# Loading the history rows of a causal convolution on a second queue, with the column shift folded into the PSUM copies and the first nodes reordered

## Chip, cores, metric

One core of one Trainium2 chip. The metric is device time in microseconds (us) of one execution; lower is better. Each kernel was run several times, and the profiled execution's length is called its span. A program on one core has no neighbour die to compare with, so every run listed here counts as a normal, fast one.

## The reference

`x` is 8 x 4096 x 512 and `kernel` 8 x 512 x 512, both fp32. The output is a causal convolution whose taps are matrices:

```python
for k in range(K):                     # K = 8
    shifted = x if k == 0 else np.concatenate(
        [np.zeros((B, k, D)), x[:, :-k, :]], axis=1)
    out += np.matmul(shifted, kernel[k])
```

## The kernel before

The 32768 rows are laid out as 128 partitions with runs of 256 consecutive rows. A block is eight rows of every run. The eight taps are not multiplied one by one: a three-level Karatsuba-like scheme splits a block into nodes LO, HI and MID and works with sums of rows (VectorE, in bf16) and differences of weights, so that TensorE has few products to do. At full clock a 128x128x512 matmul takes 0.216 us from start to start (1391 of them fill the 300 us from 100 to 400 us of the profile), and four make one "product".

The first block needs, besides its own rows, the seven rows before each run: the *history*. They are the last seven rows of the run in the partition before. The kernel before loads them already moved by one partition, with a cast to bf16 in GpSimd's DMA, and clears partition 0:

```python
def load(out, src):
    nc.gpsimd.dma_start(out=out, in_=src)          # "L80": casts fp32 -> bf16
...
H = D421
def load_h(a, b):
    load(H[1:P, 8 + a:8 + b], xr[0:P - 1, RUN + a:RUN + b, :])
load_h(-4, 0)
load_x(0, 0)
...
nc.vector.memset(H[0:1], 0.0)
...
load_w(4)
load_h(-7, -4)
...
transpose_pe("h0", 0, H, 4, 6)                     # through TensorE into PSUM
transpose_pe("x0", 2, xin[0, 0], 0, 2)
nc.vector.tensor_copy(out=XF[:, 4:6], in_=bank["x0"])
nc.vector.tensor_copy(out=XF[:, 0:2], in_=bank["h0"])
```

Later blocks come in through `load_x` (GpSimd, into one of two `xin` buffers) and `transpose_x` (a DMA transpose on SyncE's queue). A buffer of `xin` is free again when its transpose has read it, so the time of a transpose sets the time of a later load. The transpose in turn waits for VectorE to have read the old contents of `XT` (among others in `prep_d27`).

The first nodes, 0 to 5, do the first two blocks in an order of their own and are written out by hand, followed by the loop from node 6 on. The parts that matter later:

```python
mpool = ctx.enter_context(tc.tile_pool(name="m", bufs=2))       # two "ms" buffers
...
def node_e(n, b_):
    p = n.p[b_]
    if n.k < 4:                      # blocks 0 and 1: LO and HI come first, MID is added later
        pool, name = ((ypool, "y"), (mpool, "ms"), (ypool, "y"), (fpool, "f"))[n.k]
        y = pool.tile([P, 2, D], f32, name=name)
        nc.scalar.copy(out=y, in_=p)
        first[n.i, n.a, b_] = y      # summed and stored from this buffer by node_y and store
    elif n.a == MID:                 # the loop: MID comes first and is kept in ms
        ms[b_] = mpool.tile([P, 2, D], f32, name="ms")
        nc.scalar.copy(out=ms[b_], in_=p)
    ...
```

So node 1's results stay in the two `ms` buffers until their stores, of 512 KB each, have landed. The first `ms` copy of the loop (node 6) must wait for the first of those stores.

In the profile, L76 is the helper of all VectorE sums, L80 GpSimd's load.

## Time and profile before

| quantity | before |
|---|---|
| time, median of 3 runs | 782.44 us (782.19 to 783.35) |
| span of the profiled execution | 779.7 us |
| TensorE busy | 767.2 us |
| VectorE busy | 660.4 us |
| first product | at 13.44 us |

A kernel whose TensorE is busy 98% of the span can gain only where TensorE stands still or its granted clock (1.00 is full speed) is lowered. A line of the timeline gives start, length, engine, line, what; in brackets the idle time before it and what ended it. The table by stretches of the kernel before (from:to, length, then busy us and instructions of PE, PEld, DVE, ACT and POOL, then TensorE's clock, the DMA share and GB/s):

```profile
60.00:100.00 40.00, 39.95 (x185) 17.73 (x184) 38.37 (x48) 14.71 (x25) 1.58 (x3) 1.00 0.77 202
```

TensorE is full there. But the timeline of the same stretch (start, length, engine, line, what; in brackets the idle time before it and what ended it) has one transfer with little to spare:

```profile
77.29 0.33 SPq L276 DMA_DIRECT2D out_dram<-ms  x1
...
77.67 0.53 POOL L80 DMA_DIRECT2D xin<-in_x_dram  x1 [14.40 <-DMA XT<-xin]
...
82.18 1.01 ACT L293 COPY ms<-pp 128x1024 f32<-128x1024 f32 x1 [1.11 <-PE pp L191]
```

The store of `ms` is issued at 77.29, the load of a coming block 0.4 us **behind** it at 77.67. The view of transfers for 74.8 to 79 us says how long the store took (name, queue, count, KB each, us from issue to landing):

```profile
out_dram<-ms SPq DMA_DIRECT2D x1, 512.0 KB, 4.8
```

It landed at 77.29 + 4.8 = 82.1 us, and the copy that takes over the buffer starts at 82.18. By the profile this copy's last wait was for TensorE, not for the store; but a store landing more than 0.1 us later would have held it up.

### The profile page before, as it was taken

What the parts mean: (1) busy time and instruction counts of PE and PEld (TensorE: products, weight loads), DVE (VectorE), ACT (ScalarE), POOL (GpSimd) and SP (SyncE); (2) the same over time, 40 slices, a digit from 0 to 9 for tenths busy, and PEclk for the clock granted to TensorE, in tenths of its full rate; (3) what the DMA queues carried; (4) which work ended last, traced back from release to release, by engine and by line L of the source; (5) the groups of instructions that cost most, each with busy time, mean ns of one, the idle gap of its engine ahead of it and who ended that gap; (6) DMA issues with size and microseconds to landing.
All of it is one profiled execution on the core that took longest, in us unless ns stands there. A gap on an engine that the chain in (4) does not pass through costs nothing.

```text
span 779.7 us, 9419 instructions
## 1 busy us (share of the span) xinstructions
PE 767.2 (98%) x3576; PEld 347.6 (45%) x3576; DVE 660.4 (85%) x768; ACT 280.8 (36%) x459; POOL 41.8 (5%) x80
## 2 busy tenths in 40 slices
PE   6999999999999999999999999999999999999997
PEld 3444444444444444444444444444444444444443
DVE  3999988898888898888898888888888898888895
ACT  1453443324343333343333343333343333343332
POOL 4000000000000000000000000000000000000000
PEclk8999999999999999999999999999999999999999
DMA  9946888777788777687788787878697867688843
GB/s 162 210 80 169 236 189 189 186 168 178 171 176 203 176 180 180 168 193 185 166 192 176 170 198 178 198 161 185 166 190 181 202 162 186 165 186 179 205 131 124
DMA packets 159229, 138.37 MB, mean 177 GB/s; under 512 B 130130, under 2 KB 134226, under 8 KB 159184
## 3 DMA queue, kind: packets, MB, share of 16 engines
q1 hardware_dynamic: 145312, 98.84, 46.0%
q0 software_dynamic: 13728, 38.66, 30.9%
q8 instruction: 28, 0.46, 0.2%
q10 hardware_dynamic: 144, 0.26, 0.1%
q14 instruction: 17, 0.14, 0.1%
HBM read 77.32 MB, written 67.11 MB: 185 GB/s over the span
## 4 chain that ended last, share of the span: by engine, by line
PE 93%; DVE 5%; DMA 1%; issue 1%; ACT 0%; POOL 0%; DVEq 0%; POOLq 0%
PE pp L191 93%; DVE w L76 3%; DVE D L76 1%; DMA xin<-in_x_dram 1%; PE pp L180 0%; DVE pp L76 0%; DVE XT L375 0%; DVE F L76 0%; ACT D L341 0%; ACT D L342 0%; DVE D L334 0%; DVE y L76 0%; DVE pp L266 0%; POOL D L80 0%; DVEq L628 0%
## 5 line engine op out<-in xcount | busy, mean ns | idle before, releaser
L191 PE MATMUL pp<-w,D 128*128 128x512 bf16 x3280 | 718.1, 380 | 1.5 <-ACT D L342 1.1
L191 PEld LDWEIGHTS <-D 128*128 128x128 bf16 x3280 | 320.7, 98 | 391.5 <-issue 4.1
L76 DVE TENSOR_TENSOR D<-D 128x1024 bf16<-128x1024 bf16 x252 | 228.3, 945 | 0.4 <-issue 0.2
L76 DVE TENSOR_TENSOR y<-pp,ms 128x1024 f32<-128x1024 f32 (+1 forms) x121 | 146.2, 1211 | 45.3 <-PE pp L191 45.3
L76 DVE TENSOR_TENSOR D<-XT 128x2048 bf16<-128x2048 bf16 (+2 forms) x153 | 142.3, 945 | 12.2 <-DMA XT<-xin 11.0
L238 ACT COPY pp<-pp 128x512 f32<-128x512 f32 x95 | 54.1, 570 | 254.8 <-PE pp L191 254.8
L250 ACT COPY pp<-pp 128x512 f32<-128x512 f32 x95 | 54.2, 571 | 164.2 <-PE pp L191 154.5
L76 DVE TENSOR_TENSOR pp<-dts,pp 128x512 f32<-128x512 f32 x95 | 65.5, 689 | 43.1 <-ACT dts L256 41.8
L293 ACT COPY ms<-pp 128x1024 f32<-128x1024 f32 x60 | 61.0, 1016 | 33.8 <-PE pp L191 32.8
L80 POOL DMA_DIRECT2D xin<-in_x_dram x64 | 33.9, 530 | 688.0 <-DMA XT<-xin 672.8
L266 DVE SCALAR_TENSOR_TENSOR pp<-pp,dts 128x512 f32<-128x512 f32 x95 | 65.8, 693 | 3.3
L256 ACT COPY dts<-pp 128x512 f32<-128x512 f32 x95 | 57.5, 606 | 4.2 <-PE pp L191 4.2
L252 ACT ACTIVATE pp<-pp 128x512 f32<-128x512 f32 x95 | 56.0, 589 | 2.1 <-DVE D L76 2.1
L191 PE MATMUL pp<-w,XT 128*128 128x512 bf16 x120 | 30.8, 379 | 0.0
L76 DVE TENSOR_TENSOR w<-w,w 128x2048 bf16<-128x2048 bf16 x19 | 22.6, 1218 | 0.0
L191 PEld LDWEIGHTS <-XT 128*128 128x128 bf16 x120 | 11.7, 98 | 14.2
L191 PE MATMUL pp<-w,w 128*128 128x512 bf16 x36 | 9.2, 379 | 0.7 <-ACT pp L250 0.7
L191 PE MATMUL pp<-w,F 128*128 128x512 bf16 x36 | 8.6, 379 | 0.0
L174 PE MATMUL pp<-zero 128*128 128x512 bf16 x16 | 5.6, 501 | 1.2 <-DVE zero L145 1.2
L180 PE MATMUL pp<-ident,xin 128*128 128x128 bf16 x48 | 3.3, 219 | 3.3 <-DMA xin<-in_x_dram 1.9
L334 DVE COPY D<-pp 128x1024 bf16<-128x1024 bf16 x1 | 0.7, 692 | 6.7 <-PE pp L180 6.7
L80 POOL DMA_DIRECT2D w<-in_kernel_dram x8 | 6.0, 758 | 3.0 <-DMA w<-in_kernel_dram 1.9
(52 smaller groups left out, 68.9 us busy)
## 6 DMA issues: line engine op xcount, KB each, us to landing
out_dram<-y SPq DMA_DIRECT2D x123, 512.0 KB, 3.2
xin<-in_x_dram POOLq DMA_DIRECT2D x64, 512.0 KB, 5.7
w<-in_kernel_dram POOLq DMA_DIRECT2D x8, 512.0 KB, 17.2
out_dram<-ms SPq DMA_DIRECT2D x2, 512.0 KB, 6.0
out_dram<-f SPq DMA_DIRECT2D x2, 512.0 KB, 8.4
XT<-xin SPq DMA_TRANSPOSE x61, 6.1
D<-in_x_dram POOLq DMA_DIRECT2D x1, 508.0 KB, 5.5
D<-in_x_dram POOLq DMA_DIRECT2D x1, 381.0 KB, 11.3
```

The lines of the kernel that those rows point to most:

```text
L76: nc.vector.tensor_tensor(out=o, in0=a, in1=b, op=op)
L80: nc.gpsimd.dma_start(out=out, in_=src)
L174: nc.tensor.matmul(pw[:, h], lhsT=zero[:, 0:P], rhs=zero, start=True, stop=True)
L180: nc.tensor.transpose(o[:, t - t0, c * P:(c + 1) * P], src[:, t, c * P:(c + 1) * P], ident)
L191: nc.tensor.matmul(bank, lhsT=comp[:, c * P:(c + 1) * P], rhs=w[:, c, :], start=start and c == 0, stop=c == DC - 1, skip_group_check=True)
L238: nc.scalar.copy(out=n.q[:, 0], in_=n.q[:, 1])
L250: nc.scalar.copy(out=n.p[b_][:, 1], in_=n.q[:, 1])
L252: nc.scalar.mul(out=n.p[b_][:, 1], in_=n.q[:, 1], mul=-1.0)
L256: nc.scalar.copy(out=n.dts, in_=n.q[:, 0])
L266: nc.vector.scalar_tensor_tensor(out=p[:, 0], in0=p[:, 1], scalar=-1.0, in1=n.dts, op0=MUL, op1=SUB)
L293: nc.scalar.copy(out=ms[b_], in_=p)
L334: nc.vector.tensor_copy(out=XF[:, 4:6], in_=bank["x0"])
```

## The change

The intent is a shorter opening. The history's four nearest rows go to SyncE's free queue, so that GpSimd can issue `x` first. That queue's load here stays fp32, so the cast moves to VectorE and ScalarE. The rows are loaded into the same partition that they lie in (no offset, no clearing of partition 0), and the move to the next column is made while the transposes are copied out of PSUM. The order of the hand-written part, nodes 0 to 6, is redone as well. The loop is untouched. The core of the diff, cuts marked:

```diff
-    H = D421
-    def load_h(a, b):
-        load(H[1:P, 8 + a:8 + b], xr[0:P - 1, RUN + a:RUN + b, :])
-    load_h(-4, 0)
+    H, HF = XT, D421.bitcast(f32).rearrange("p (t b) d -> p t (b d)", b=2)
+    nc.sync.dma_start(out=HF, in_=xr[:, RUN - 4:RUN, :])
     load_x(0, 0)
 ...
-    nc.vector.memset(H[0:1], 0.0)
 ...
-    load_h(-7, -4)
+    load(H[:, 1:4], xr[:, RUN - 7:RUN - 4, :])
 ...
+    def to(z):
+        return z.rearrange("p t (c m) -> p t c m", m=P)[:, :, :, 1:P]
+    def prev(z):
+        return z.rearrange("p t (c m) -> p t c m", m=P)[:, :, :, 0:P - 1]
 ...
-    transpose_pe("h0", 0, H, 4, 6)
+    nc.vector.tensor_copy(out=H[:, 4:6], in_=HF[:, 0:2])
+    nc.scalar.copy(out=H[:, 6:8], in_=HF[:, 2:4])
+    n0.p = {0: pair(0), 1: pair(1)}
+    load_w(6)
+    transpose_pe("h0", 3, H, 4, 6)
+    transpose_pe("h1", 0, H, 6, 8)
+    nc.scalar.copy(out=to(XF[:, 0:2]), in_=prev(bank["h0"]))
+    first_run(XF[:, 0:2])
     transpose_pe("x0", 2, xin[0, 0], 0, 2)
-    nc.vector.tensor_copy(out=XF[:, 4:6], in_=bank["x0"])
-    nc.vector.tensor_copy(out=XF[:, 0:2], in_=bank["h0"])
-    first_run(XF[:, 0:2])
+    nc.scalar.copy(out=XF[:, 4:6], in_=bank["x0"])
 ... (the order of the rest of nodes 0 to 3)
-    node_d(nodes[5], 0)
-    prep_d27()
-    node_seed(nodes[5], 1)
-    node_v(nodes[5], 1)
 ...
+    node_seed(nodes[5], 1)
+    node_y(nodes[4], 1, LO)
+    prep_d27()
+    node_d(nodes[5], 0)
+    node_v(nodes[5], 1)
+    node_d(nodes[5], 1)
 ...
     node_a1(6)
-    node_d(nodes[5], 1)
+    node_l(nodes[5], 0, LO)
+    node_a0(nodes[6])
+    load_x(3, 1)
     transpose_x(2, 1)
 ...
     store(1, LO, 0, first[1, LO, 0])
 ...
-    load_x(3, 1)
 ...
```

More of the change, by code (lines that the diff above doesn't have):

```diff
@@ L333 @@
+    transpose_pe("h1", 0, H, 6, 8)
+    nc.scalar.copy(out=to(XF[:, 0:2]), in_=prev(bank["h0"]))
+    first_run(XF[:, 0:2])
     transpose_pe("x0", 2, xin[0, 0], 0, 2)
-    nc.vector.tensor_copy(out=XF[:, 4:6], in_=bank["x0"])
-    nc.vector.tensor_copy(out=XF[:, 0:2], in_=bank["h0"])
-    first_run(XF[:, 0:2])
+    nc.scalar.copy(out=XF[:, 4:6], in_=bank["x0"])
     tt(D4[:, 0:2], XF[:, 0:2], XF[:, 4:6], ADD)
-    transpose_pe("xb", 2, xin[0, 0], 2, 4)
-    n0.p = {0: pair(0), 1: pair(1)}
-    transpose_pe("h1", 0, H, 6, 8)
@@ L341 @@
-    nc.scalar.copy(out=XF[:, 6:8], in_=bank["xb"])
-    nc.scalar.copy(out=XF[:, 2:4], in_=bank["h1"])
+    load_w(5)
+    transpose_pe("xb", 3, xin[0, 0], 2, 4)
+    nc.scalar.copy(out=to(XF[:, 2:4]), in_=prev(bank["h1"]))
     direct(0, 0)
+    nc.vector.tensor_copy(out=XF[:, 6:8], in_=bank["xb"])
     first_run(XF[:, 2:4])
-    load_w(6)
-    transpose_pe("he", 2, H, 1, 4)
-    load_w(5)
+    fill(pair(3))
+    transpose_pe("he", 1, H, 1, 4)
     tt(D4[:, 2:4], XF[:, 2:4], XF[:, 6:8], ADD)
+    load_w(7)
@@ L349 @@
+    load_x(0, 1)
+    tt(D2, XF[:, 1:6], XF[:, 3:8], ADD)
+    direct(0, 2)
     direct(0, 3)
+    load_x(1, 0)
+    tt(to(E4[:, 1:4]), prev(bank["he"]), to(XF[:, 1:4]), ADD)
+    direct(2, 2)
     direct(0, 1)
-    nc.scalar.copy(out=F0, in_=XF[:, 4])
-    fill(pair(3))
-    direct(0, 2)
-    direct(2, 2)
-    tt(E4[:, 1:4], bank["he"], XF[:, 1:4], ADD)
-    first_run(E4[:, 1:4])
-    tt(D2, XF[:, 1:6], XF[:, 3:8], ADD)
-    load_w(7)
-    direct(1, 0)
-    direct(1, 3)
-    load_x(0, 1)
+    first_run(E4[:, 1:4])
@@ L362 @@
+    direct(1, 1)
     tt(D1, XF[:, 3:5], XF[:, 4:6], ADD)
-    direct(1, 2)
     mid_dve(1, LO, HI)
-    load_x(1, 0)
-    direct(1, 1)
+    nc.vector.tensor_copy(out=F0, in_=XF[:, 4])
     mid_dve(2, LO, HI)
     tt(F21, D2[:, 0:4], D2[:, 1:5], ADD)
+    direct(2, 0)
+    mid_dve(2, LO, LO)
+    load_w(2)
+    mid_dve(1, LO, LO)
     load_w(0)
-    mid_dve(1, LO, LO)
-    mid_dve(2, LO, LO)
+    direct(1, 3)
     direct(2, 3)
     mid_dve(2, LO, MID)
+    direct(1, 0)
     transpose_pe("x1", 2, xin[0, 1], 0, 4)
@@ L376 @@
     tt(D4[:, 4:8], XF[:, 4:8], XT[:, 4:8], ADD)
-    direct(2, 0)
-    nc.scalar.copy(out=C0[:, 0:2], in_=XT[:, 6:8])
+    direct(1, 2)
+    tt(D42[:, 3], D4[:, 1], D4[:, 3], ADD)
+    transpose_pe("x2", 2, xin[1, 0], 0, 4)
     prep_d41(HI)
-    transpose_pe("x2", 2, xin[1, 0], 0, 4)
-    nc.scalar.copy(out=XT[:, 2:4], in_=bank["x2"][:, 2:4])
-    load_w(2)
-    direct(3, 0)
-    prep_d42(HI)
+    direct(3, 2)
     nc.scalar.copy(out=XT[:, 0:2], in_=bank["x2"][:, 0:2])
     direct(3, 3)
+    nc.scalar.copy(out=XT[:, 2:4], in_=bank["x2"][:, 2:4])
@@ L387 @@
+    nc.scalar.copy(out=C0[:, 0:2], in_=XT[:, 6:8])
+    nc.scalar.copy(out=C1, in_=XT[:, 0:4])
+    prep_d42(HI)
     tt(T4, XT[:, 4:8], XT[:, 0:4], ADD)
+    direct(3, 0)
+    fill(pair(2))
     direct(3, 1)
-    fill(pair(2))
+    tt(D41[:, 1], T4[:, 0], T4[:, 1], ADD)
     load_w(3)
-    nc.scalar.copy(out=C1, in_=XT[:, 0:4])
-    direct(3, 2)
-    tt(D41[:, 1], T4[:, 0], T4[:, 1], ADD)
     node_a1(1)
+    direct(2, 1)
+    node_u(nodes[1])
     tt(D41[:, 0], D4[:, 7], T4[:, 0], ADD)
-    direct(2, 1)
+    tt(T42[:, 0:2], D4[:, 6:8], T4[:, 0:2], ADD)
@@ L397 @@
+    tt(D421[:, 0], D42[:, 7], T42[:, 0], ADD)
+    tt(T42[:, 2:4], T4[:, 0:2], T4[:, 2:4], ADD)
+    mid_dve(1, HI, HI)
     load_w(1)
-    node_a0(nodes[1])
-    tt(T42[:, 0:2], D4[:, 6:8], T4[:, 0:2], ADD)
-    tt(T42[:, 2:4], T4[:, 0:2], T4[:, 2:4], ADD)
-    node_u(nodes[1])
-    load_x(1, 1)
-    tt(D421[:, 0], D42[:, 7], T42[:, 0], ADD)
-    node_e(nodes[0], 0)
+    node_e(nodes[0], 0)
+    load_x(1, 1)
+    load_x(2, 0)
+    prep_d27()
+    mid_dve(2, HI, LO)
+    node_a0(nodes[1])
     node_seed(nodes[1], 0)
-    mid_dve(1, HI, HI)
@@ L407 @@
-    prep_d27()
     node_v(nodes[1], 0)
-    mid_dve(2, HI, LO)
+    node_dts(nodes[1])
     tt(D421[:, 1:4], T42[:, 0:3], T42[:, 1:4], ADD)
+    node_d(nodes[1], 0)
     node_seed(nodes[1], 1)
-    node_dts(nodes[1])
-    tt(D42[:, 3], D4[:, 1], D4[:, 3], ADD)
-    load_x(2, 0)
-    node_d(nodes[1], 0)
     mid_dve(1, HI, LO)
+    node_e(nodes[0], 1)
     mid_dve(2, HI, HI)
-    node_a1(2)
+    node_v(nodes[1], 1)
+    mid_dve(2, HI, MID)
     node_l(nodes[1], 0, HI)
-    node_v(nodes[1], 1)
     load_x(2, 1)
@@ L422 @@
     node_d(nodes[1], 1)
-    mid_dve(2, HI, MID)
     prep_d421(HI)
+    mid_dve(0, HI, HI)
+    node_a1(2)
     node_l(nodes[1], 0, LO)
+    node_e(nodes[1], 0)
+    transpose_x(1, 1)
     node_a0(nodes[2])
-    node_l(nodes[1], 1, HI)
-    node_e(nodes[1], 0)
-    node_e(nodes[0], 1)
-    nc.scalar.copy(out=D4[:, 2:4], in_=T4[:, 2:4])
-    node_u(nodes[2])
-    mid_dve(0, HI, HI)
-    node_seed(nodes[2], 0)
+    node_u(nodes[2])
+    node_l(nodes[1], 1, LO)
+    node_seed(nodes[2], 0)
+    prep_d4(HI)
@@ L434 @@
+    nc.scalar.copy(out=D4[:, 2:4], in_=T4[:, 2:4])
+    node_l(nodes[1], 1, HI)
     node_seed(nodes[2], 1)
-    node_l(nodes[1], 1, LO)
     node_dts(nodes[2])
-    transpose_x(1, 1)
+    node_v(nodes[2], 0)
+    node_d(nodes[2], 0)
+    node_e(nodes[1], 1)
+    node_v(nodes[2], 1)
+    node_l(nodes[2], 0, HI)
     nc.scalar.copy(out=D42[:, 3], in_=T42[:, 3])
-    node_v(nodes[2], 0)
-    node_v(nodes[2], 1)
-    prep_d4(HI)
     prep_d41(HI)
-    node_d(nodes[2], 0)
+    mid_dve(0, LO, LO)
+    nc.scalar.copy(out=U1, in_=XT[:, 0])
@@ L444 @@
     node_a1(3)
     node_l(nodes[2], 0, LO)
-    mid_dve(0, LO, LO)
-    mid_dve(0, HI, LO)
-    prep_d42(HI)
-    node_l(nodes[2], 0, HI)
-    node_a0(nodes[3])
-    node_d(nodes[2], 1)
-    node_u(nodes[3])
-    node_e(nodes[2], 0)
-    node_e(nodes[1], 1)
-    node_seed(nodes[3], 0)
+    node_d(nodes[2], 1)
+    node_a0(nodes[3])
+    node_e(nodes[2], 0)
+    prep_d42(HI)
+    node_l(nodes[2], 1, LO)
+    node_u(nodes[3])
+    node_seed(nodes[3], 0)
+    node_l(nodes[2], 1, HI)
+    mid_dve(0, HI, LO)
@@ L456 @@
+    node_seed(nodes[3], 1)
     tt(D421[:, 0:4], D42[:, 3:7], D42[:, 4:8], ADD)
-    node_l(nodes[2], 1, HI)
-    node_seed(nodes[3], 1)
+    node_e(nodes[2], 1)
+    node_dts(nodes[3])
     mid_dve(0, LO, HI)
+    node_v(nodes[3], 1)
     tt(A1[:, 0], C0[:, 1], C1[:, 0], ADD)
-    node_dts(nodes[3])
+    mid_dve(1, MID, HI)
     node_v(nodes[3], 0)
-    node_v(nodes[3], 1)
-    mid_dve(1, MID, HI)
-    node_l(nodes[2], 1, LO)
     node_d(nodes[3], 1)
-    node_e(nodes[2], 1)
     node_d(nodes[3], 0)
-    mid_dve(1, MID, LO)
@@ L470 @@
     node_a1(4)
     node_l(nodes[3], 1, HI)
+    mid_dve(1, MID, LO)
     node_l(nodes[3], 0, LO)
-    nc.scalar.copy(out=U1, in_=XT[:, 0])
     node_a0(nodes[4])
+    node_l(nodes[3], 0, HI)
+    node_dts(nodes[4])
     tt(D21[:, 2:4], C1[:, 0:2], C1[:, 2:4], ADD)
     mid_dve(2, MID, MID)
-    node_dts(nodes[4])
     tt(D21[:, 0:2], C0[:, 0:2], C1[:, 0:2], ADD)
-    node_l(nodes[3], 0, HI)
-    node_e(nodes[3], 0)
-    node_u(nodes[4])
     tt(A1[:, 1], C1[:, 0], C1[:, 1], ADD)
-    node_l(nodes[3], 1, LO)
@@ L486 @@
     mid_dve(2, MID, LO)
+    node_e(nodes[3], 0)
+    node_u(nodes[4])
     node_seed(nodes[4], 0)
+    mid_dve(2, MID, HI)
+    node_l(nodes[3], 1, LO)
     node_seed(nodes[4], 1)
     node_v(nodes[4], 0)
-    mid_dve(2, MID, HI)
+    node_e(nodes[3], 1)
+    node_d(nodes[4], 0)
     node_a1(5)
-    node_d(nodes[4], 0)
     node_v(nodes[4], 1)
     node_l(nodes[4], 0, HI)
+    node_l(nodes[4], 0, LO)
+    node_u(nodes[5])
     prep_m()
-    node_l(nodes[4], 0, LO)
-    node_e(nodes[3], 1)
-    node_u(nodes[5])
+    node_a0(nodes[5])
@@ L499 @@
+    node_seed(nodes[5], 0)
     node_d(nodes[4], 1)
-    node_a0(nodes[5])
     node_y(nodes[4], 0, LO)
+    tt(F21[:, 0], D2[:, 0], D21[:, 0], ADD)
     node_y(nodes[4], 0, HI)
+    node_l(nodes[4], 1, LO)
     prep_d4(LO)
     node_l(nodes[4], 1, HI)
-    tt(F21[:, 1], D21[:, 0], D21[:, 1], ADD)
-    node_dts(nodes[5])
-    tt(F21[:, 0], D2[:, 0], D21[:, 0], ADD)
-    node_seed(nodes[5], 0)
-    node_l(nodes[4], 1, LO)
-    node_v(nodes[5], 0)
-    node_y(nodes[4], 1, LO)
-    store(0, LO, 0, first[0, LO, 0])
@@ L513 @@
-    store(0, HI, 0, first[0, HI, 0])
-    node_d(nodes[5], 0)
-    prep_d27()
-    node_seed(nodes[5], 1)
-    node_v(nodes[5], 1)
+    node_dts(nodes[5])
+    node_v(nodes[5], 0)
+    store(0, LO, 0, first[0, LO, 0])
+    node_seed(nodes[5], 1)
+    node_y(nodes[4], 1, LO)
+    prep_d27()
+    node_d(nodes[5], 0)
+    node_v(nodes[5], 1)
+    node_d(nodes[5], 1)
+    store(0, HI, 0, first[0, HI, 0])
+    tt(F21[:, 1], D21[:, 0], D21[:, 1], ADD)
+    node_y(nodes[4], 1, HI)
     node_a1(6)
-    node_d(nodes[5], 1)
+    node_l(nodes[5], 0, LO)
@@ L520 @@
+    node_a0(nodes[6])
+    load_x(3, 1)
     transpose_x(2, 1)
-    node_y(nodes[4], 1, HI)
-    store(0, HI, 1, first[0, HI, 1])
-    node_l(nodes[5], 0, HI)
-    node_l(nodes[5], 0, LO)
-    tt(F21[:, 2:4], D21[:, 1:3], D21[:, 2:4], ADD)
-    node_y(nodes[5], 0, HI)
-    node_u(nodes[6])
+    node_l(nodes[5], 0, HI)
+    store(0, LO, 1, first[0, LO, 1])
+    node_u(nodes[6])
+    tt(F21[:, 2:4], D21[:, 1:3], D21[:, 2:4], ADD)
+    prep_d41(LO)
+    node_y(nodes[5], 0, HI)
+    node_l(nodes[5], 1, LO)
@@ L528 @@
+    node_seed(nodes[6], 0)
+    store(0, HI, 1, first[0, HI, 1])
     node_y(nodes[5], 0, LO)
-    prep_d41(LO)
+    node_v(nodes[6], 0)
     node_l(nodes[5], 1, HI)
-    node_l(nodes[5], 1, LO)
-    store(0, LO, 1, first[0, LO, 1])
-    node_seed(nodes[6], 0)
-    node_a0(nodes[6])
-    node_v(nodes[6], 0)
+    store(1, LO, 0, first[1, LO, 0])
+    node_dts(nodes[6])
+    store(1, HI, 0, first[1, HI, 0])
     tt(D21[:, 0:2], D2[:, 0:2], D2[:, 1:3], ADD)
-    store(1, LO, 0, first[1, LO, 0])
+    node_d(nodes[6], 0)
@@ L538 @@
+    node_y(nodes[5], 1, HI)
+    node_y(nodes[5], 1, LO)
     node_seed(nodes[6], 1)
     node_v(nodes[6], 1)
-    node_dts(nodes[6])
-    prep_d42(LO)
-    node_d(nodes[6], 0)
-    store(1, HI, 0, first[1, HI, 0])
-    node_y(nodes[5], 1, HI)
-    node_a1(7)
-    load_x(3, 1)
-    node_y(nodes[5], 1, LO)
-    store(1, HI, 1, first[1, HI, 1])
-    store(1, LO, 1, first[1, LO, 1])
     tt(D21[:, 2:4], D2[:, 2:4], D2[:, 3:5], ADD)
     node_d(nodes[6], 1)
+    prep_d42(LO)
+    store(1, HI, 1, first[1, HI, 1])
@@ L552 @@
+    node_a1(7)
     prep_d4(HI)
+    store(1, LO, 1, first[1, LO, 1])
     for k, (i, a) in enumerate(order):
```

## The prediction

> **What bounds the kernel now.** I read the page first, then the table by stretches of the span, then the timeline and the chain of waits of the first 60 us, because the change touches nothing after that: from the loop on the two programs issue the same instructions in the same order.
>
> The page:
>
> ```profile
> span 779.7 us, 9419 instructions
> PE 767.2 (98%) x3576; PEld 347.6 (45%) x3576; DVE 660.4 (85%) x768; ACT 280.8 (36%) x459; POOL 41.8 (5%) x80
> ...
> PE   6999999999999999999999999999999999999997
> ...
> PEclk8999999999999999999999999999999999999999
> DMA  9946888777788777687788787878697867688843
> ```
>
> TensorE is full in 38 of 40 slices. Only the first slice (19.5 us) has idle TensorE and a lowered clock, and there the DMA engines are already at 9 tenths. So the end can move only by what the opening loses. The table by stretches says where that is (per stretch: length, then busy us and instructions of PE, PEld, DVE, ACT, POOL, then TensorE clock, DMA share, GB/s):
>
> ```profile
> 5.00:10.00 5.00, 1.81 (x19) 1.06 (x18) 0.02 (x1) 0.00 (x0) 2.08 (x4) 1.00 1.07 194
> 10.00:13.44 3.44, 1.61 (x17) 1.33 (x17) 2.08 (x4) 2.07 (x3) 1.72 (x3) 0.70 1.13 196
> 13.44:16.00 2.56, 2.56 (x13) 1.44 (x13) 0.81 (x2) 0.46 (x1) 1.07 (x2) 0.50 1.17 186
> 18.00:20.00 2.00, 2.00 (x10) 0.93 (x9) 2.00 (x4) 0.00 (x0) 0.18 (x1) 0.95 1.24 205
> 25.00:30.00 5.00, 4.36 (x45) 2.78 (x44) 4.93 (x6) 1.93 (x2) 1.08 (x2) 1.00 1.17 202
> 35.00:40.00 5.00, 4.34 (x20) 1.76 (x19) 5.00 (x7) 2.92 (x5) 0.00 (x0) 1.00 1.13 215
> ```
>
> Up to 13.44 us there is no product at all; then TensorE is continuous at half clock until about 18.2, and later loses 0.64 and 0.66 us in the stretches from 25 and from 35. From 60 us to 760 us it loses 0.05 us. The chain of waits of the opening (start, length, what) tells what holds the first product back:
>
> ```profile
> 1.25 0.66 POOL D L80
> 1.91 7.37 DMA xin<-in_x_dram
> 9.28 0.05 issue
> 9.32 0.64 PE pp L180 x8
> ...
> 9.98 0.70 DVE D L334
> ...
> 11.37 1.01 ACT D L341
> 12.38 1.01 ACT D L342
> ...
> 13.44 1.87 PE pp L191 x4
> ```
>
> GpSimd first issues the history rows (0.66 us of its time), then x; x lands at 9.28; then transposes, a VectorE copy, transposes, two ScalarE copies of 1.01 us in a row, and the first product. The history itself landed before (5.5 us after its issue at 1.25, so 6.75). The first weight, issued at 2.44, landed 10.3 us later, at about 12.74, 0.7 us before it was used. And two gaps later on, in the timeline:
>
> ```profile
> 28.03 1.05 PE L180 MATMUL pp<-ident,xin 128*128 128x128 bf16 x16 [0.64 <-DVE XT L375]
> 37.10 1.02 PE L191 MATMUL pp<-w,w 128*128 128x512 bf16 x4 [0.66 <-ACT pp L250]
> ```
>
> **What the Trainium skill says.** "DMA: Bandwidth & Descriptors", section "Issuing engines are not separate DMA queues": DMAs of all issuers run on the same 16 DMA engines and interleave; a second issuer saves only sequencer time. The trace of before has one issuer here, with the engines at a share of about 1.1 from 4.5 us on, so it agrees that they are the scarce thing and cannot show the interleaving. The same page, "SWDGE vs HWDGE vs iDMA": a cast inside a DMA is for GpSimd's queue alone, which is why SyncE's load must stay fp32 and needs a cast on chip. "TensorE: Matmul & The Clock Gate", "What's actually happening": the clock is set by free-running windows of 3413 ns and returns to full after about one busy window. The trace agrees: a mean of 0.70 over 10 to 13.44 puts the drop at 11.38 (1.0 for 1.38 us, 0.5 for 2.06), 0.95 over 18 to 20 puts the return at 18.2, which is 6.8 us or two windows later. "SBUF — State Buffer", "Who interferes with whom": a VectorE copy in a two-port mode, which a cast from fp32 in SBUF is, keeps GpSimd from writing descriptors; no operation of before in the opening shows it, and GpSimd's early issues end at 7.08 (6.51 + 0.57), about when the cast would start.
>
> **The change part by part.**
>
> *Queue.* One GpSimd issue goes: x moves from 1.91 to 1.25, 0.66 us earlier, and every later load with it. SyncE has been free since 0.7, so the history issues at about 0.75, 0.5 us earlier than now. Volume: from the spacing of landings (6.75, 9.28, 12.74, and 3.18 + 11.3 = 14.48 for the rest of the history) 1 MB of fp32 read takes some 2.5 to 3.4 us. The fp32 load reads the same 1 MB; it writes twice the bytes, and I take reading as what counts, since the engines sustain about 205 GB/s written with fp32 read, so 410 GB/s read. My estimates: the history lands between 6.3 and 8 (it now shares with x), x at about 8.7, the first weight at about 12.1, and the later ones 0.6 us earlier than now.
>
> *Casts.* Added: a VectorE copy 128x1024 fp32 to bf16 and a ScalarE copy of the same size, side by side. ScalarE takes 1.01 (row L341); VectorE about 0.7 (row L334 has the same element count at two per cycle). Removed: the 1.76 us VectorE memset of one partition, which lay beside the DMA and cost nothing.
>
> *Transposes and shift.* The column shift rides in the copies of the transposes, 128x8x127 in place of 128x1024: no extra instruction, 1.01 us each on ScalarE. The sum of two history rows from PSUM also becomes 12x127: I take it at its old 0.96 us.
>
> *The new path to the first product.* History at 7.0, cast to 8.05 (ScalarE), second transposes 8.4 to 9.05, ScalarE copy of the first bank 8.45 to 9.45, x transposes to 9.7, ScalarE copies of x and of the second bank 9.7 to 11.7. The second bank is the bank the first product writes, so it waits for that copy: 11.75. The first weight at 12.1 comes later, so the first product starts at about 12.1 to 12.2: 1.25 us earlier than 13.44.
>
> *What of it survives to the end.* Eleven products plus fillers and transposes lie before the transposes of the third x tile in both versions, so TensorE is ready for it at 28.03 - 0.64 - 1.25 = 26.1. But its load landed at about 27.5 before and would land at 26.9: start 26.9, a gain of 1.1. After that the reordering matters: VectorE's T4 sum ends earlier relative to TensorE, which removes the 0.34 us wait for D41 at 32.8; and the product by U is put ahead of the one whose seed it feeds, so that ScalarE's seed copy (0.57 us) lies beside a product of 0.86 us, which should remove most of the 0.66 us gap at 37.1. VectorE's own chain, busy for all of 35 to 40, starts its dense part earlier too (its copies went to ScalarE; it was idle 2.1 us up to 16.62), by about 1.2 to 1.5 us, so it does not hold this back by more than some tenths. I count 1.1 + 0.3 + 0.5 = 1.9, less 0.2 for new small waits: 1.7 us. 782.44 - 1.7 = 780.7 us.
>
> **The rivals.**
>
> 1. DMA is the wall. If the loads do not advance (the fp32 write of twice the bytes eats the 0.66 us), the third x tile lands at 27.5 as before and most of the start is given back as a wait there. For it: DMA share above 1.0 without a break, and TensorE already waiting 0.32 us for xin at 25.46. Against: GpSimd's queue loses 1 MB to read and starts 0.66 us sooner. Then the gain is 0.5 plus perhaps 0.5 of gaps: 781.5.
> 2. The history comes late. SyncE's and GpSimd's packets alternate, both x and history finish at about 8.7, ScalarE's four operations in a row (cast, three copies, 4 us) then end at 12.7 to 13, and the gain at the first product is 0.5. Against it: the history starts alone for about half a microsecond. Then 781.4 to 782.
> 3. The clock. TensorE's window grid is where it is. With a product from 12.1, the window 11.38 to 14.79 is busy for 80% and more in place of some 65%; if that counts as busy, the clock returns 3.4 us earlier, worth 1.7 us of TensorE time. Of this the loads would give back most, as the second x tile lands only at about 24.8. A phase that falls badly costs as much. Up to 1 us either way: 779.7 to 781.7.
> 4. VectorE stays the bound of 17 to 55 us, with the strided sum at one element per cycle (1524 / 0.96 = 1.59 + 0.16 = 1.75 us, 0.8 more). Then 781.5.
>
> **Range and chances.** The middle of the sum is 780.7. The rivals for less put it at 781.4 to 782, the favourable clock at 779.7 or a little below; three runs of before spread over 1.2 us by themselves. An 80% range is 779.2 to 782.1. For a change of 2% the time would have to move by 15.6 us, more than the whole 13.44 us before the first product; nothing I see costs or saves that. Faster by over 2%: 0.005, within: 0.99, slower: 0.005.
>
> **What would show it.** In the timeline of after: the history's transfer issued on SyncE's queue near 0.75 and the first transposes near 7.7 to 8.5; the first product near 12.2, and what it waited for (the weight: my path; a ScalarE copy: rival 2); the start of the third tile's transposes near 26.9, waiting for its load (if it is 27.5, rival 1); the TensorE idle time before 37 without the 0.34 and 0.66 us waits; the clock by stretches (a return well before 18 is rival 3); the duration of the 12x127 sum (1.7 us is rival 4). Beyond 60 us everything should be as before, shifted. I am wrong in kind if the first product comes at 12.2 and the end doesn't move, or if the end moves by over 3 us.

## More of the kernel before

Of the lines of before, L180 is a TensorE transpose, L191 a product's matmul, L238, L250 and L252 are ScalarE copies that seed PSUM banks, L293 the `ms` copy, L276 a store and L89 the DMA transpose. In the kernel after all but L76, L80 and L89 are one less or so (L179, L190, L237, L249, L251, L292, L275).

Only the second `ms` copy waits for a store, the second one, and TensorE doesn't stop for that:

```profile
89.83 1.01 ACT L293 COPY ms<-pp 128x1024 f32<-128x1024 f32 x1 [0.96 <-DMA out_dram<-ms]
```

## The result

The kernel after is correct and takes **784.49 us** (median of 4 runs, 783.40 to 785.83) against 782.62 us (median of 4) for before. The ratio is 1.0024, with a 95% interval of 1.0002 to 1.0046: it is slower by 0.2%, where 0.2% faster was predicted. Ratios here are the mean time of one kernel's fast runs over the mean of the other's fast runs in the same rounds, so they aren't quite the ratio of the quoted medians. Two later series of the kernel after (below) gave 1.0032 and 1.0041.

The page of the kernel after:

```profile
span 781.4 us, 9358 instructions
...
PE   7899899999999999999999999999999999999997
...
PEclk9999999999999999999999999999999999999999
```

The first slice is fuller (7 for 6) and the clock is never lowered in this execution, yet the span is 781.4 - 779.7 = 1.7 us longer. TensorE's row has two digits of 8 where before had 9. The second slice (19.5 to 39 us) is the opening's waiting for loads, at a full clock. The fifth, 78 to 98 us, is new: nothing of the opening is left there. (TensorE's busy total is not compared: 71 of its 3576 matmul records are missing from this trace.)

The opening in the timeline of the kernel after:

```profile
0.74 0.39 SPq L142 DMA_DIRECT2D D<-in_x_dram  x1
...
5.58 0.91 DVE L337 CAST XT<-D 128x1024 bf16<-128x1024 f32 x1 [4.44 <-DMA D<-in_x_dram]
...
8.09 1.07 PE L179 MATMUL pp<-ident,xin 128*128 128x128 bf16 x16 [0.47 <-DMA xin<-in_x_dram]
...
11.42 1.02 PE L190 MATMUL pp<-w,D 128*128 128x512 bf16 x4 [2.27 <-DVE D L331]
...
14.08 0.96 DVE L76 TENSOR_TENSOR w<-pp,D 128x1524 bf16<-128x1524 bf16 x1 [0.59 <-PE pp L179]
...
26.99 1.05 PE L179 MATMUL pp<-ident,xin 128*128 128x128 bf16 x16 [0.45 <-DVE XT L383]
...
36.20 2.02 PE L190 MATMUL pp<-w,w 128*128 128x512 bf16 x8 [0.66 <-ACT pp L249]
```

The history lands at 5.54 us (4.8 after its issue at 0.74), the x tile at about 8.05 instead of 9.28, and the first product starts at 11.42 instead of 13.44. The third x tile's transposes start at 26.99 instead of 28.03. The stretch up to 13.44 us, where before had a clock of 0.70 (the third number from the end; here it is 1.00):

```profile
10.00:13.44 3.44, 1.49 (x10) 0.77 (x12) 3.24 (x5) 0.67 (x1) 1.50 (x3) 1.00 1.12 196
```

At about 59 us TensorE is ahead: the product with F starts at 58.76 us against 59.97 in before, so 1.21 us are won. A part of that is the clock: over the first 20 us it averaged 1.00 in this profile and 0.83 in before's. In a later profile of the same kernel (after_third) it was 0.83 too, and there the product with F starts at 59.72, only 0.25 us ahead of before. Then comes the loss. The table by stretches of the kernel after:

```profile
60.00:100.00 40.00, 36.78 (x168) 16.37 (x169) 35.76 (x44) 12.98 (x22) 1.06 (x2) 1.00 0.69 171
```

36.78 us busy where before had 39.95: 3.17 us less, nearly all of it in one place. The chain of waits through that stretch names the cause:

```profile
76.67 8.23 DMA out_dram<-ms
...
86.54 7.50 PE pp L190 x34
```

Everything hangs on the `ms` store, 8.23 us of pure waiting. The timeline of the kernel after, with the same three events as shown for before, and the matmul that had to wait:

```profile
75.34 0.53 POOL L80 DMA_DIRECT2D xin<-in_x_dram  x1 [21.94 <-DMA XT<-xin]
...
76.67 0.33 SPq L275 DMA_DIRECT2D out_dram<-ms  x1
...
84.99 1.01 ACT L292 COPY ms<-pp 128x1024 f32<-128x1024 f32 x1 [5.12 <-DMA out_dram<-ms]
...
86.54 13.98 PE L190 MATMUL pp<-w,D 128*128 128x512 bf16 x63 [3.02 <-ACT pp L249]
```

The load is now issued 1.3 us **ahead** of the store instead of 0.4 us behind it. The store took 8.2 us instead of 4.8:

```profile
out_dram<-ms SPq DMA_DIRECT2D x1, 512.0 KB, 8.2
```

ScalarE was ready for the `ms` copy at 84.99 - 5.12 = 79.87 us and got the buffer 5.12 us later; the seed of a PSUM bank (L249) stands behind that copy in ScalarE's order; TensorE stands still for 3.02 us (so some 2.1 of the 5.12 us were slack). The sum: 1.21 won, 3.02 lost, 1.8 us net, against 1.7 in the spans.

### The profile page after: what moved, and what is told of

Same layout as the page of the kernel before. It is cut to its first block, busy times and chain, and to the rows that moved or that the text cites. A ratio compares the mean times of both kernels' runs of the same rounds, so it can differ in the third digit from the quotient of the medians.

```text
span 781.4 us, 9358 instructions
## 1 busy us (share of the span) xinstructions
PE 761.4 (97%) x3505; PEld 346.3 (44%) x3576; DVE 659.6 (84%) x768; ACT 281.9 (36%) x460; POOL 41.3 (5%) x79
## 4 chain that ended last, share of the span: by engine, by line
PE 90%; DVE 4%; DMA 3%; issue 1%; POOL 1%; ACT 0%; DVEq 0%; ACTq 0%; POOLq 0%
PE pp L190 90%; DMA xin<-in_x_dram 2%; DVE D L76 1%; DVE w L76 1%; DMA out_dram<-ms 1%; DVE y L76 1%; POOL w L80 0%; DVE pp L76 0%; DVE pp L265 0%; ACT pp L249 0%; DVE F L76 0%; DVE XT L383 0%; DVE ms L76 0%; DVE f L76 0%; PE pp L179 0%
## 5 line engine op out<-in xcount | busy, mean ns | idle before, releaser
L76 DVE TENSOR_TENSOR D<-D 128x1024 bf16<-128x1024 bf16 (+1 forms) x252 | 228.4, 946 | 1.4 <-ACT D L346 1.2
L249 ACT COPY pp<-pp 128x512 f32<-128x512 f32 x95 | 54.2, 570 | 170.9 <-PE pp L190 161.7
L292 ACT COPY ms<-pp 128x1024 f32<-128x1024 f32 x60 | 61.0, 1017 | 37.1 <-PE pp L190 30.9
L190 PEld LDWEIGHTS <-w 128*128 128x128 bf16 x36 | 3.5, 98 | 5.0 <-issue 1.2
```

Source lines behind the costliest of these rows:

```text
L76: nc.vector.tensor_tensor(out=o, in0=a, in1=b, op=op)
L190: nc.tensor.matmul(bank, lhsT=comp[:, c * P:(c + 1) * P], rhs=w[:, c, :], start=start and c == 0, stop=c == DC - 1, skip_group_check=True)
L249: nc.scalar.copy(out=n.p[b_][:, 1], in_=n.q[:, 1])
```

## The experiments

**Theory.** The opening gains about what was predicted. The new *order* of nodes 4 to 6 puts the load of block 3 ahead of the `ms` store, the store then takes 8 us instead of 5, and the `ms` buffer comes free too late.

**Rivals.** (1) The opening itself is to blame: TensorE arrives 1.2 us earlier at a buffer that comes free when it always did. (2) The order matters, but through some other wait, and the buffer is only where it shows. (3) The granted clock: the standstill or the new opening changes when TensorE's clock is lowered, and that makes the difference.

All kernels below gave correct results. The medians are of 5 runs (gap_filled: 6; after_again: 4), each with the kernel before measured on the same chip: 782.75 us (first four kernels), 782.83 (next four) and 782.60 (last three).

### Splitting the change: new opening alone, new order alone

One kernel takes the new opening and the new order up to `node_a0(nodes[4])`, and the old order from there to the loop; the other takes the old opening and the new order from there on.

```diff
 # head_new = after, with from here to the loop the text of before:
     node_a0(nodes[4])
-    node_l(nodes[3], 0, HI)
-    node_dts(nodes[4])
     tt(D21[:, 2:4], C1[:, 0:2], C1[:, 2:4], ADD)
     mid_dve(2, MID, MID)
+    node_dts(nodes[4])
 ...
 # tail_new = before, with from here to the loop the text of after
```

> The new opening (loads, casts, shift, order up to the first product of node 4 by A) with the old order from there on. Theory: keeps the 1.2 us won in the opening and, with the transpose and the next x load at their old place behind the y stores, loses 0 to 0.8 us at the ms copy: 781.4 to 782.2. Rival (the opening itself is what costs, by the clock): 783.5 or more.

> The old opening with the new order from node 4 on. Theory: no gain in the opening, and the ms copy waits as in the changed kernel, since there too the x load is issued ahead of the ms store: a TensorE gap of 2.5 to 3 us near 87 us, 785 to 785.6. Rival (the gap came from the opening being earlier, not from the order): gap under 1 us, 782.6 to 783.3.

Measured: the new opening with the old order takes **780.59 us** (780.09 to 781.63), ratio 0.9974 [0.9961, 0.9986]. The old opening with the new order takes **786.78 us** (785.47 to 788.13), ratio 1.0052 [1.0039, 1.0064]. In the first, the load is issued 0.5 us behind the `ms` store (76.11 and 75.61), the store lands after 4.8 us, the copy behind it last waits for TensorE as in before, and TensorE is busy for all of 75 to 90 us:

```profile
75.00:90.00 15.00, 15.00 (x71) 6.73 (x70) 14.19 (x19) 5.83 (x9) 0.53 (x1) 1.00 0.89 271
```

In the second, the load is 1.3 us ahead (77.52 and 78.80), the store takes 8.6 us and ScalarE waits 5.5. Against before, with TensorE 0.9 us later at the product with F (60.88 for 59.97), the store went out 1.5 us later and the load 0.15 us earlier (77.52 for 77.67): the new order moves both. The profile is of the slowest of the five executions (788.13 us). Its timeline and, below it, its table by stretches:

```profile
89.06 15.67 PE L191 MATMUL pp<-w,D 128*128 128x512 bf16 x64 [3.42 <-ACT pp L250]
```

```profile
90.00:92.00 2.00, 2.00 (x7) 0.74 (x6) 1.00 (x2) 0.01 (x1) 0.00 (x0) 0.52 0.69 151
```

Both medians lie outside what was expected, the first 0.8 us below, the second 1.2 us above, and on the side of the theory in each. The two halves add up: -2.2 us for the opening and +4.0 us for the order make +1.9, and the whole change measured +1.9 in its first series. Rival 1 falls, since an equally early TensorE loses nothing with the old order. The cost of the order is larger than the standstill: right behind it, the granted clock was 0.52 between 90 and 92 us, and 64 matmuls took 15.67 us where 64 x 0.216 = 13.8 would do. That part of rival 3 is true and comes on top.

### Taking away the buffer that waits

In node 6 the first `ms` goes into a tile that is dead by then (F21, of the same size), so that the late store holds nobody. Done to both kernels:

```diff
-            ms[b_] = mpool.tile([P, 2, D], f32, name="ms")
+            if n.k == 6 and b_ == LO:
+                ms[b_] = F21.bitcast(f32).rearrange("p (t b) d -> p t (b d)", b=2)
+            else:
+                ms[b_] = mpool.tile([P, 2, D], f32, name="ms")
```

> The changed kernel with one edit: the first ms tile of the loop (node 6, first half) lies in F21, which is dead by then, so its copy no longer waits for the store of the ms tile before it. Theory (new wait): the 3.0 us TensorE gap at 83.5 to 86.5 us goes; the time falls by 2.5 to 3 us against the changed kernel, to about 781.4 (some 1.2 us under before). Rival (clock only): the gap goes but the time stays at 783.4 to 785.8, since lowered clock and not the wait is what costs. Rival (the wait moves): another copy waits for the next store, the gap stays above 1.5 us and the time above 783.

> The kernel before with the same edit. In its profile the same copy waited 1.0 us for the store but TensorE had no gap there. Theory: no change, 782.6 within 0.4. Rival (the store's wait costs before as well, through ScalarE): 0.7 to 1 us faster.

Measured: after with this edit takes **780.88 us** (779.73 to 782.04), ratio 0.9976 [0.9963, 0.9990]; before with it 782.49 us (782.17 to 783.14), ratio 0.9998 [0.9985, 1.0011]. The store still takes 8.4 us, but nobody waits for it, and TensorE is busy for all of 75 to 90 us. So the wait for this one buffer accounts for the whole loss, and rival 2 falls for the part that reaches TensorE; before, which has no such standstill, gains nothing. (The expectation for before had the 1.0 us wait on "the same copy"; it was on the second one, which the edit frees too.)

### Moving the load back behind the store

That the *order of load and store* is what makes the store slow was so far an inference. In the next kernel the new order stays, but GpSimd first reads one element that VectorE's last sum into `ms` has written, and issues the load only then. The transpose stays early.

```diff
-    load_x(3, 1)
     transpose_x(2, 1)
 ...
     node_y(nodes[5], 0, LO)
+    tick = spool.tile([1, 1], f32, name="tick")
+    nc.gpsimd.tensor_copy(out=tick, in_=first[1, LO, 0][0:1, 0, 0:1])
+    load_x(3, 1)
```

> The changed kernel; GpSimd first reads one element of the ms tile (after its last sum on VectorE, near 76.6 us) and only then issues the x load that went out at 75.34. Theory (the x load ahead of the ms store is what makes the store land late): the store lands in about 5 us in place of 8.2, the ms copy waits 1 to 2 us in place of 5.1, TensorE's gap is under 0.5 us, the time 780.9 to 781.6. Rival (the store is slow by itself, or by the f stores behind it): lands in 8 us still, gap 3 us, time 783.4 or more.

Measured: **780.14 us** (779.85 to 780.58), ratio 0.9966 [0.9954, 0.9979], 0.8 us below the expected range and the lowest median (the interval overlaps that of the new opening with the old order). The view of transfers (74.8 to 79 us) and the timeline of this kernel:

```profile
out_dram<-ms SPq DMA_DIRECT2D x1, 512.0 KB, 3.5
```

```profile
76.63 0.33 SPq L275 DMA_DIRECT2D out_dram<-ms  x1
...
77.19 0.53 POOL L80 DMA_DIRECT2D xin<-in_x_dram  x1
...
80.96 1.01 ACT L292 COPY ms<-pp 128x1024 f32<-128x1024 f32 x1 [1.15 <-PE pp L190]
```

Issued at 77.19 instead of 75.34, the load is now 0.6 us behind the store (76.63), the store lands in 3.5 us instead of 8.2, and the `ms` copy's last wait is for TensorE, as in before. The store itself goes out when it did (76.67), and so do the stores of `f` right behind it (77.00 for 77.05), so neither a late store nor those explain the 8.2 us. A delay of 1.85 us of *one load*, for which nobody waits at that time, wins back everything: the time is that of the new opening with the old order (780.59), or a little better.

The other way to the same end is to move the transpose as well, behind the stores of node 1's first halves:

```diff
-    load_x(3, 1)
-    transpose_x(2, 1)
 ...
     store(1, LO, 0, first[1, LO, 0])
     node_dts(nodes[6])
     store(1, HI, 0, first[1, HI, 0])
+    load_x(3, 1)
+    transpose_x(2, 1)
```

> The changed kernel; the DMA transpose that has to end before the x load may start is moved behind the ms and the first f store in SyncE's order. Theory: the ms store then meets neither transpose nor load, lands in under 4 us, the gap goes; VectorE may wait up to 1 us for the transposed rows near 82.5. Time 780.7 to 781.8. Rival (the later transpose holds up the next node): 783 or more with a TensorE wait on XT.

Measured: 782.37 us (781.69 to 783.16), ratio 0.9996 [0.9983, 1.0010], above the expected 780.7 to 781.8. The `ms` store lands after 2.6 us and the wait for the buffer is gone, but VectorE now waits 1.8 us for the late transpose. The timeline:

```profile
86.76 8.82 PE L190 MATMUL pp<-w,D 128*128 128x512 bf16 x40 [1.18 <-DVE D L76]
```

So the transpose was early for a reason, and only the load should have been held back. The wait had been exchanged for a smaller one.

### What of the opening is the queue

The new opening changes two things: the queue (with the casts that it needs) and the shift in the copies. This kernel is the one with the new opening and the old order, but with the history loaded on GpSimd's queue as bf16, into the same partitions, without casts on chip:

```diff
-    H, HF = XT, D421.bitcast(f32).rearrange("p (t b) d -> p t (b d)", b=2)
-    nc.sync.dma_start(out=HF, in_=xr[:, RUN - 4:RUN, :])
+    H = XT
+    load(H[:, 4:8], xr[:, RUN - 4:RUN, :])
 ...
-    nc.vector.tensor_copy(out=H[:, 4:6], in_=HF[:, 0:2])
-    nc.scalar.copy(out=H[:, 6:8], in_=HF[:, 2:4])
```

> The new opening and the old tail (the run that gave 780.59), but the history rows come through GpSimd's queue as bf16, as before: no SyncE load and no casts, the shift stays. Theory (the loads are the wall of the opening, the queue change advances them by 0.66 us): the first product 0.7 to 1.3 us later, the tiles of x 0.6 to 0.9 us later, time 781.2 to 781.6. Rival (the gain is from the order and the shift alone): within 0.3 of 780.6.

Measured: 782.92 us (781.77 to 783.09), ratio 0.9997 [0.9985, 1.0010]: as slow as before, and slower than I had expected. The timeline:

```profile
12.14 1.02 PE L190 MATMUL pp<-w,D 128*128 128x512 bf16 x4 [2.12 <-DMA w<-in_kernel_dram]
```

The x tile's transposes start at 8.96 us (8.07 with SyncE's queue), and the first product at 12.14 (11.13). From there the difference grows to 1.9 us at the third x tile (28.45 against 26.51), because in this execution the clock was at half from about 13 to 20 us (0.50 over 16 to 20, where the other kernel's had 1.00). The shift and the new order of the first nodes alone gain nothing that can be told apart from the runs' spread; a gain came only with the load off GpSimd's queue. How much of the 2.3 us between the two medians is the queue and how much the clock's phase in the executions caught, one profile each can't say. The executions' mean clocks, 0.992 to 0.998 here and 0.996 to 0.999 there, point to a part of each.

### The levels of the kernel after, and the clock

In its first series the kernel after fell on two levels: 783.40 and 783.43 us at a mean clock of 1.0, and 785.55 and 785.83 at 0.993. To see more of them, it was run again, once with three rounds on the chip of the last-named kernels and once with five rounds beside a kernel made to keep TensorE busy:

> The changed kernel as it is, for a profile and more clocks. It had two levels: 783.4 at a clock of 1.0 and 785.7 at 0.993. Theory (the gap of 3 us sometimes lets TensorE's clock fall for a window or two after it): the executions fall on the same two levels, the slower ones at the lower mean clock, and if the profile falls on the slow level the clock by stretches is lowered right behind the gap, as it was in the run with the new tail alone (0.83 over 90 to 100). Rival (the clock of the opening makes the two levels): lowered clock before 20 us only.

> The kernel after once more, on the same chip as gap_filled, to be compared with it. Every theory: 783.4 to 786.6 in several levels, median near 784.9; ratio 1.002 to 1.004; the gap of about 3 us at 84 to 86.5 us, with the ms store landing after 8.2 us or more. If the profile falls on a slow level, the theory that the gap lets the clock fall expects the granted clock below 1 in the stretch right behind 86 us; the rival expects it below 1 in the first 40 us only, for longer than in the other profiles.

```diff
 # gap_filled = after, with in the loop:
+        if k == 6:
+            for _ in range(12):
+                nc.tensor.matmul(nxt.p[0][:, 0], lhsT=cur.s[3][0][:, 0:P], rhs=cur.s[3][0],
+                                 start=True, stop=True, skip_group_check=True)
         if nxt:
             for b_ in range(2):
                 node_v(nxt, b_)
```

> The kernel after with twelve spare 512-column matmuls emitted on TensorE in the seventh node, where it stands still for about 3 us; they write a PSUM buffer that the next product overwrites, so the result is unchanged. The late ms copy stays late. Theory (the standstill is what lets the granted clock fall in some executions, and so makes the levels 783.4, 784.8 and 786): all executions come near 783.4, within 782.8 to 784.2, with the mean clock at 0.995 or above; the gap ahead of the row of 63 products shrinks to under 1.5 us. Rival (the levels come from how the clock rises in the opening, as the clock's phase falls): still some executions at 785.5 to 786.6 with a clock of 0.992.

Measured: after_again 784.10 (clock 1.0), 784.83 (0.996), 786.12 (0.993) and 786.60 us (0.992), ratio 1.0032 [1.0019, 1.0046]. after_third 785.71 us (785.62 to 786.52; 784.9 had been expected), clocks 0.993 to 0.996, ratio 1.0041 [1.0028, 1.0054]. This time the profile fell on a slow level (span 784.5). From its timeline and its table by stretches:

```profile
87.83 15.67 PE L190 MATMUL pp<-w,D 128*128 128x512 bf16 x63 [3.35 <-ACT pp L249]
```

```profile
88.00:90.00 2.00, 2.00 (x6) 0.76 (x5) 0.34 (x1) 0.78 (x2) 0.00 (x0) 0.50 1.30 103
```

Against the first profile (span 781.4) nearly all of the 3.1 us is made up so: 1.0 us is lost in the opening, where the clock averaged 0.83 over the first 20 us instead of 1.00 (the product with F starts at 59.72 instead of 58.76); 0.3 us is a longer standstill (3.35 instead of 3.02); and 1.7 us is lost behind it, as the same row of 63 matmuls takes 15.67 us instead of 13.98, with the clock at 0.50. **Both** theories of the levels, the opening's clock and the fall behind the gap, hold in part. Behind standstills of 3.02 and 3.2 us (the profiles of after and after_again) the clock stayed at 1.00; behind 3.35 and 3.42 (after_third and the new order alone) it fell. But it fell behind one of only 2.96 us as well (gap_filled, below: 0.50 from 86.5 to 89 us). So the length of the standstill alone doesn't decide it.

The kernel gap_filled failed as an experiment. It took 787.56 us (785.47 to 789.87), ratio 1.0064 [1.0052, 1.0077]. The timeline shows why:

```profile
86.37 4.29 PE L594 MATMUL pp<-D 128*128 128x512 bf16 x12 [2.96 <-ACT pp L249]
```

The twelve spare matmuls write a PSUM bank that was itself waiting for the same ScalarE copy, so they stood *behind* the standstill and lengthened the path by about 4.1 us in that execution (the next product starts at 90.50), at half clock for most of it. It says nothing on what a filled gap would do; that stays open.

### The gap at 36 us

The prediction counted on most of a 0.66 us wait at 37.1 us going away. The kernel after still has it, at 36.20. In its timeline the seed copy (L249) waits until the a0 product ahead of it in the order has ended. So, on top of the fastest kernel:

```diff
-    node_a0(nodes[1])
     node_seed(nodes[1], 0)
+    node_a0(nodes[1])
     node_v(nodes[1], 0)
```

> The kernel late_load with, besides, the seed of the second node emitted ahead of the four a0 products of that node instead of behind them. Theory (the 0.66 us that TensorE waits at 36.2 us in the kernel after is the seed copy waiting for the last a0 product that was emitted ahead of it, which the change could not touch): that wait falls under 0.2 us, and the time to 779.4 to 779.9, against 780.1 of late_load. Rival (the wait is the ScalarE copy's own length, or another wait takes its place at once): the wait stays above 0.5 us, here or a little later, and the time stays at 780.0 to 780.4.

Measured: 780.79 us (780.62 to 781.18), ratio 0.9978 [0.9966, 0.9990]. It isn't faster than the kernel that it was built on (0.9966 [0.9954, 0.9979]), and 0.4 us above what even the rival expected. The seed no longer waits for the a0 product (it starts at 35.25 without idle time), but TensorE's wait has only moved:

```profile
35.88 1.02 PE L190 MATMUL pp<-w,D 128*128 128x512 bf16 x3 [0.73 <-ACT pp L249]
```

The a0 product now waits 0.73 us for the seed copy, and a 0.30 us wait on the next seed follows at 38.07. The rival of this experiment was right: another wait takes the place of this one at once. In both orders TensorE stands until that ScalarE copy has ended.

## Why the prediction was wrong

Its point estimate was 780.7 us with a range of 779.2 to 782.1; 784.49 lies above it. Step by step:

- **History on SyncE's queue, x and weights earlier: right in direction, too cautious in size.** History landed at 5.54 us (predicted 6.3 to 8), x at 8.05 (8.7), the first weight at about 11.3 (12.1). With twice the bytes written, the load took 4.8 us against the 5.5 of before; it also had the engines to itself at first.
- **Casts: VectorE under-sized.** 0.91 us, not 0.7: the fp32 source is not copied at the rate of the bf16 copy from PSUM that I took it from (0.70). ScalarE took 1.05 (1.01). It cost nothing, as the cast was done at 6.5 us and x came at 8.05. The issue on GpSimd that lay beside the cast took 0.68 us for 0.57, so a lock-out of GpSimd cost at most 0.1 us.
- **First product: earlier than predicted.** 11.42 instead of 12.1 to 12.2. In this profile it waited for VectorE's clearing of 64 columns, which ended about when the weight landed; in the later two of the same kernel (11.57 and 11.63) it waited for the weight, as predicted.
- **Third x tile at 26.9: the number right, the wait not** (26.99, a gain of 1.04 us for 1.1 predicted). The load landed at 26.66, and the transposes waited for VectorE's copy out of PSUM (the 0.45 us in the line shown), as in before (0.64), where the load had landed at 27.53. The loads took much of the early start back, but at the second x tile, where TensorE waited 1.58 us in this full-clock profile.
- **12x127 sum: right.** 0.96 us, as before; rival 4 falls. (Its 1.75 us can be worked out from before's timeline as an estimate: VectorE takes 0.69 us for 1024 elements and 1.22 for 2048; at half that rate 1524 would take about 1.74.)
- **The two gaps: wrong.** The 0.34 us at 32.8 was a wait of the weight loads (PEld); TensorE was busy for 5.00 of the 5.00 us from 30 to 35, so there was nothing to win, and in the kernel after the same wait is 0.48 us (at 31.91). The 0.32 us at 25.46 in rival 1 was misread the same way. The wait of 0.66 us is still there. (And the page's first slice is not the only one with idle TensorE: the last one, with a digit of 7, has it in both kernels.) I had read the order (the product by U put ahead), but not that the a0 product also stands ahead of the seed; and the last experiment shows that moving it doesn't help. Of 1.7 us predicted, 1.21 are there at 59 us, with a clock that was better than before's.
- **The step that failed**: "from the loop on the two programs issue the same instructions in the same order", and with it "Beyond 60 us everything should be as before, shifted". Of the loop that is true. But the last nodes before the loop, up to about 77 us, were reordered as well, and I had taken the stretch from 60 us on for untouched because TensorE was full there in before. The new order put a load 1.3 us ahead of a store that had been 0.4 us ahead of it. The store's 4.8 us became 8.2; the `ms` copy, which in before had waited for TensorE and not for this store, waited 5.12 us for it, and TensorE lost 3.02 us. The parts tell it apart: opening alone 780.59, where the prediction said 780.7 (in part by luck, as the 0.6 us counted for the gaps did not come); order alone +4.0 us; the load moved back 780.14.
- **Rival 3, the clock: underrated in two ways.** Its favourable case came in part: over the first 20 us the clock averaged 0.83 in before's profile, 0.91 with the opening alone and 1.00 in after's, and the mean clock was 0.993 to 0.996 in all 29 executions of before beside these kernels, 0.996 to 0.999 in the five of the opening alone. How much of the opening's 2.2 us is the clock and how much the loads, no run separates. And I had looked for it in the opening only. The new standstill brought a second fall of the clock in some executions, worth 1.7 us in the profile that caught it.
- I had named as a case "wrong in kind" that the first product comes early and the end doesn't move. Something like it came (the end moved the other way), and the first 60 us of the profile could not have shown it.

## What to carry to other kernels

When a change reorders a hand-made schedule, its effect is not confined to the stretch that it was meant for: list every buffer whose release is a DMA (here a pool of two behind a 512 KB store), read its slack from the profile of before, and compare where the issues of loads and stores fall relative to each other. A load that is issued earlier than anybody needs it isn't free: here one load moved from 0.4 us behind a store to 1.3 us ahead of it cost 3.0 us of TensorE time, and holding it back by 1.85 us won all of it. Split such a change at a point where both orders agree and run the halves.

## What the Trainium skill lacked or had wrong

- "DMA: Bandwidth & Descriptors", section "Issuing engines are not separate DMA queues", says that transfers of different issuers interleave and that a second issuer only saves sequencer time, usually little. The runs agree on the interleaving. What the page lacks is what it can cost: a 512 KB store on SyncE's queue landed after 3.5 to 4.8 us with a 512 KB load from GpSimd 0.3 to 0.6 us behind it, and after 8.2 to 8.6 us with that load 1.3 us ahead.
- The same section calls the saving in sequencer time usually small relative to the DMA itself. The sizes agree (0.66 us of issue, 6.8 us for the load of x); what it lacks is that at the head of a kernel that waits for loads the saving is passed on. Here the transposes of the first x tile came 0.9 us earlier with the history on SyncE's queue, and the medians of the two kernels differ by 2.3 us (780.59 and 782.92), a part of which is the clock's phase.
- "TensorE: Matmul & The Clock Gate", section "What's actually happening", has the clock fall after at least one idle window of about 3.4 us. Here it also fell behind a standstill of 2.96 us, in which no such window fits whole, while it did not fall behind 3.02 and 3.2 and did behind 3.35 and 3.42. Such a fall cost 1.7 us beyond the standstill in after_third.
